# A mixer's output gates as one token-stationary block of 1024 columns

## The chip, the cores and the metric

The kernel runs on one core of a Trainium2 chip. The metric is the device time of one execution, in microseconds. The core has a matrix engine (TensorE, PE in the profile, with its weight loads as PEld), a vector engine (VectorE, DVE), a scalar engine (ScalarE, ACT), a fourth engine (GpSimd, POOL) and DMA queues that SyncE (SP) feeds. Products accumulate in PSUM and are read out by VectorE or ScalarE.

## The reference, cut to what matters

One encoder layer in fp32 over 256 tokens of width 2048: a half-step SwiGLU, a mixer, a cross-attention to 256 memory tokens, another half-step SwiGLU, a final norm. The change lies in the mixer alone:

```python
h = rms_norm(x, mix_norm[l])
proj = h @ w_in[l]                       # 2048 x 4112
u, q, k, v, g, a_lr = jnp.split(proj, list(IN_SPLITS), axis=-1)
y_pool = pool_mixer(u, pool_w[l], pool_scale[l])
y_gla = gla_mixer(q, k, v, g, a_lr, gla_w_a2[l], gla_b_a[l], gla_head_norm[l])
x = x + jnp.concatenate([y_pool, y_gla], axis=-1) @ w_out[l]
...
def gla_mixer(q, k, v, g, a_lr, w_a2, b_a, head_norm):
    ...                                  # 4 heads: scores over chunks of 64 frames, o = scores @ v
    o = o * lax.rsqrt(jnp.mean(o * o, axis=-1, keepdims=True) + RMS_EPS)
    o = o.reshape(b, s, D_GLA) * head_norm.astype(jnp.float32)
    return o.astype(dt) * jax.nn.silu(g)
```

The gates `g` are 1024 columns of `proj`, 256 for each of four heads. A head's normed output, times its gain, is multiplied by silu of its gates and becomes one eighth of the input of `w_out`.

## The kernel before, in words

**Numbers.** Every large product is made of three: weights and activations are split into a high part (`wh`, or `xh`; the first of the two parts in `xs` and `ys`) and a low part (`wl`, `xl`). For each tile of weights ScalarE casts the high part (L1607) and VectorE subtracts it to get the low part (L453, inside `low_parts`). `xs` holds the normed input of the mixer, `ys` the input of `w_out`, both as 16 tiles of 128 rows of the feature axis by 256 tokens, in two parts.

**The weight stream.** The class `Stream` keeps a list of units (one load of 1 MB of weights with its products) and of operations between them. `st.op(f, n)` puts `f` behind the n-th unit from there, or at once for n = 0. `emit` splits the weights of a unit two units ahead. Weight splits on VectorE and ScalarE keep their order (`in_turn`); other work is put among them by a list scheduler, which also moves ready instructions past others that wait.

**Forms of a block.** `block_a` (512 columns) keeps weights in the array and streams tokens: for each tile of 128 rows and each 128 columns one product of 512 columns (`wh` against both parts of the activations) and one of 256 (`wl` against the high part), both on L347. The result is transposed: features on partitions. `block_s` (1024 columns) keeps tokens in the array and streams 512 columns of weights: a pair of 128-row tiles takes 24 products of 512 columns (`unit_p`, L362), or, for the pairs in its sums, seven block products in place of eight, that is 21 (`seven`, L507). Such a pair needs more splitting: `split_seven` (L486, L280, L489, L453). Its result has tokens on partitions. Behind its last seven, `combine` (L574 to L579) adds the partial sums out of PSUM, and behind its last unit `join` (L589) adds the rest. Rows that have to have features on partitions are turned by `rows_turned` (L780): eight transposes for 512 columns.

**PSUM.** There is one pool of four tiles of two banks each (`ptile`). `block_s` holds two over the block (`open_whole`) and two more between its first seven and `combine` (`open_parts`).

**The order around the change.** Queries and keys (a `block_s`), the forget gate (`a_unit`), pool columns (two `block_a`), values V (a `block_s`, sevens at pairs 1 and 3, with `scores` of heads 0 and 1 behind its first two units), the pool group's own product (`pool_unit`, L1025), then the gates as two `block_a`. In between stand the heads' steps: `scores(h)` (decayed queries `QD`, L1155 and L1157; products, L1165; copies, L1171), `attend(h)` (L1178, L1181, L1187, L1189), `head_squares`, `head_norms(b)` (L1200) and `head_scale(b)` (L233, L1214) for each two heads. `ev_g` evicts the gates of a head: `joined` (L318, L319, L323), silu (L1221), the product with the head's output (L1223) and the split into `ys` (L285, L286). Then the block of `w_out` begins: pairs 1, 2, 3, 5, 0, 6, 4, 7 of `ys`, with sevens at pairs 0 and 4. Heads 0 to 3 are pairs 4 to 7.

Of the kernel before, what the change touches and what calls it, by code (L numbers as in the profile page):

```python
# [7 lines left out]
F32 = mybir.dt.float32  # L8
F32R = mybir.dt.float32r
AF = mybir.ActivationFunctionType  # L10
ALU = mybir.AluOpType
# [3 lines left out]
P = 128  # L15
D = 2048
S = 256
# [3 lines left out]
NB = 512  # L21
CH = 64
H = 4
# [7 lines left out]
G_FFN1, G_MIX, G_X, G_MEM, G_FFN2, G_PS, G_HN, G_BA, G_END = 0, 16, 32, 48, 64, 80, 88, 96, 100  # L31
# [68 lines left out]
def build(ctx, tc, I, out):  # L100
    nc = tc.nc
    st = Stream()
# [7 lines left out]
    scope = {"stack": None}  # L110
# [34 lines left out]
    def uid(s):  # L145
        cnt[0] += 1
        return f"{s}{cnt[0]}"

    def ctile():
        return scope["pool"].tile([P, 2, S], F32, tag="c", name=uid("c"), bufs=2)  # L150

    def ttile():
        return shared_tile("t", 2 * S, F32, uid("t"), 3).rearrange("p (a b) -> p a b", a=2)
# [27 lines left out]
    Rcol = ctl("Rcol", [P, 2])  # L181
# [8 lines left out]
    xs = main.tile([P, KT, 2, S], F32R, tag="xs", name="xs")  # L190
    ys = main.tile([P, KT, 2, S], F32R, tag="ys", name="ys")

    def gcol(i):
        return gains[:, i : i + 1]
# [102 lines left out]
    diag, rows = {}, {}  # L297
# [17 lines left out]
    def joined(ps, dst, scale=None, first=False):  # L315

        c = ctile()
        nc.scalar.copy(c, ps[:, :, S:])  # L318
        add = nc.vector.tensor_tensor(out=dst, in0=ps[:, :, :S], in1=c, op=ALU.add)  # L319
        if first:  # L320
            latest["vector"] = add
        if scale is not None:
            nc.vector.tensor_tensor(out=dst, in0=dst, in1=bc(scale), op=ALU.mult)  # L323
# [307 lines left out]
    def wblock(w, n0, k0=0, nk=KT):  # L631

        def src(k):
            return lambda raw: wload(raw.rearrange("p (k n) -> p k n", n=NB), w, k, 4, n0)
        return [src(k0 + k) for k in range(0, nk, 4)]
# [3 lines left out]
    def wwide(w, n0, k0=0, nk=KT):  # L639

        def src(k):
            def load(raw):
                raw = raw.rearrange("p (k n) -> p k n", n=2 * NB)
                if len(loaded) < 3:
                    for kk in range(2):
                        parts = (0, NB) if not loaded else (0,)
                        for c in parts:
                            n = 2 * NB // len(parts)
                            wload(raw[:, kk : kk + 1, c : c + n], w, k + kk, 1, n0 + c, n)
                else:  # L650
                    wload(raw, w, k, 2, n0, 2 * NB)
                next(first_loads, None)
                loaded.append(1)
            return load
        return [src(k0 + k) for k in range(0, nk, 2)]
# [119 lines left out]
    def rows_turned(g):  # L775

        v = four(ptile(uid("ph")))
        for i in range(4):
            for h in range(2):
                nc.tensor.transpose(  # L780
                    v[:, i, h * P : (h + 1) * P], g[:, h, i * P : (i + 1) * P], ident
                )
        return v
# [170 lines left out]
    w_in = I["w_in"][0]  # L954
    mix = {}

    def mt(name, shape, tag=None, bufs=1):
        t = whole_lines(scope["pool"], shape, F32, tag or name, uid(name), bufs)
        mix[name] = t
        return t  # L960
# [12 lines left out]
    def m4():  # L973
        return scope["pool"].tile([P, 2 * 2 * (S + PAD)], F32, tag="m4", name=uid("m4"), bufs=3)
# [164 lines left out]
        return mix["v"][:, 2 * (1 - j) + t, at : at + P]  # L1139

    def score_tile(h):
        s = mix["ST", h] = ctile() if h % 2 else mt("ST", [P, 2, S], "wa2")
        nc.gpsimd.memset(s[64:128, 0, 0:CH], 0.0)
        nc.gpsimd.memset(s[64:128, 1, 2 * CH : 3 * CH], 0.0)
        return s

    def scores(h):
        q, kd, E, F = mix["q"][:, h, :], mix["k"][:, h, :], mix["E"], mix["F"]
        e = lambda c: E[:, 4 * h + c : 4 * h + c + 1]
        f = lambda i: F[:, i, h : h + 1]  # L1150
        QD = scope["pool"].tile([P, 3 * NB], F32, tag=("xh", "xl")[h % 2], name=uid("QD"), bufs=1)
        at = (0, 3 * CH, 5 * CH)
        factors = {(0, 1): e(1), (0, 2): f(0), (0, 3): f(2), (1, 2): e(2), (1, 3): f(1), (2, 3): e(3)}
        for j in range(3):
            nc.scalar.copy(QD[:, at[j] + j * CH : at[j] + (j + 1) * CH], q[:, j * CH : (j + 1) * CH])  # L1155
            for c in range(j + 1, 4):
                nc.vector.tensor_scalar_mul(  # L1157
                    QD[:, at[j] + c * CH : at[j] + (c + 1) * CH], q[:, c * CH : (c + 1) * CH],
                    factors[j, c],
                )  # L1160
        ps = ptile(uid("pq"))
        for j in range(4):
            part = slice((j % 2) * CH, (j % 2 + 1) * CH)
            rhs = QD[:, at[j] + j * CH : at[j] + S] if j < 3 else q[:, 3 * CH :]
            nc.tensor.matmul(  # L1165
                ps[part, j // 2, j * CH : S], kd[:, j * CH : (j + 1) * CH], rhs, start=True, stop=True
            )
        s = score_tile(h)
        for j in range(4):
            part = slice((j % 2) * CH, (j % 2 + 1) * CH)  # L1170
            nc.vector.tensor_copy(s[part, j // 2, j * CH :], ps[part, j // 2, j * CH : S])  # L1171

    def attend(h):
        s = mix["ST", h]
        po = ptile(uid("po"))
        for vt in range(2):
            col = h * DV + vt * P
            nc.tensor.matmul(  # L1178
                po[:, vt, :S], v_part(0, col), s[:, 0, :], start=True, stop=False
            )  # L1180
            nc.tensor.matmul(  # L1181
                po[:, vt, 2 * CH : S], v_part(1, col), s[:, 1, 2 * CH :], start=False, stop=True
            )
        if h % 2 == 0:
            mix["oz", h // 2] = as_four(m4())
        q = mix["osq", h] = ttile()
        nc.scalar.activation(q, po[:, :, :S], AF.Square)  # L1187
        i = h % 2
        nc.vector.tensor_copy(mix["oz", h // 2][:, 2 * i : 2 * i + 2, :], po[:, :, :S])  # L1189

    def head_squares(h):
        sq = mix["osq", h]
        nc.vector.tensor_tensor(out=sq[:, 0, :], in0=sq[:, 0, :], in1=sq[:, 1, :], op=ALU.add)

    def head_norms(b):
        pn = ptile(uid("pn"))
        for i in range(2):
            sq = mix["osq", 2 * b + i]
            for t in range(2):
                nc.tensor.matmul(  # L1200
                    pn[:, 0, 2 * i + t : 2 * i + t + 1], sq[:, 0, t * P : (t + 1) * P],
                    ones[:, 0:1], start=True, stop=True,
                )
        r = mt("r", [P, 4])
        rsqrt(r, pn[:, 0, :4], DV, 4)
        mix["diag"] = [diagonal(r[:, i : i + 1]) for i in range(4)]

    def head_scale(b):
        ps = ptile(uid("ps"))
        for i in range(4):  # L1210
            spread(ps[:, i // 2, :], i % 2, mix["diag"][i])
        for i in range(2):
            oz = mix["oz", b][:, 2 * i : 2 * i + 2, :]
            nc.vector.tensor_tensor(out=oz, in0=oz, in1=bc(ps[:, i, :S]), op=ALU.mult)  # L1214

    def ev_g(b):
        def evict(p, ps):
            h = 2 * b + p
            t = ttile()
            joined(ps, t, rows["R"], b == 0)  # L1220
            nc.scalar.activation(t, t, AF.Silu)  # L1221
            for vt in range(2):
                nc.vector.scalar_tensor_tensor(  # L1223
                    out=t[:, vt, :], in0=mix["oz", b][:, 2 * p + vt, :], scalar=gcol(G_HN + 2 * h + vt),
                    in1=t[:, vt, :], op0=ALU.mult, op1=ALU.mult,
                )
            split_pair(ys, 8 + 2 * h, t)
        return evict

    for h in range(2):  # L1230
        st.op(lambda h=h: scores(h), 1 + h)
    block_s(wwide(w_in, 4 * NB), xs, qk_sums, (0, 2, 4, 5, 1, 6, 3, 7), ev_v, home=v_home)
    st.unit(load_pool, pool_unit)
    for g in range(4):
        st.op(lambda g=g: pool_out(g))
    for h in range(2):
        st.op(lambda h=h: attend(h), h)
        st.op(lambda h=h: head_squares(h), h)
        st.op(lambda h=h: scores(2 + h), h + 1)
        st.op(lambda h=h: attend(2 + h), h + 2)  # L1240
        st.op(lambda h=h: head_squares(2 + h), h + 2)
    for b in range(2):
        st.op(lambda b=b: head_norms(b), 2 + 2 * b)
        st.op(lambda b=b: head_scale(b), 3 + 2 * b)
    block_a(wblock(w_in, 6 * NB), xs, ev_g(0), (0, 0))
    block_a(wblock(w_in, 7 * NB), xs, ev_g(1))
    st.op(close_scope, 1)

    OUT_HOMES = {"T": [("kv", D, 2)], "xh": [("kv", D, 2), ("att", 3 * NB, 2)],
# [399 lines left out]
```

## Time and profile before

| | |
|---|---|
| median of 3 runs | 2077.93 us (2077.92 to 2078.28) |
| the profiled execution's own time | 2078.49 us |
| its span, first to last instruction | 2076.7 us |
| PE busy | 2064.0 us (99%) |
| DVE busy | 1833.9 us (88%) |
| ACT busy | 1158.5 us (56%) |
| POOL busy | 103.8 us (5%) |
| granted clock of TensorE | 0.999 |

The busy time of PE counts overlapping products, so the pace of a stretch is read from the chain of waits, whose rows give a start, a length and a count of instructions in a row. A row of a group gives what an instruction reads and writes, its shapes, its count, busy time and mean length, and then the idle time before it with what ended it. The table by stretches gives each engine's busy time between two moments, with its count of instructions.

### The profile page before, as it was taken

To read this page: it belongs to the slowest core of one execution; us is meant where nothing else is said; L and a number is where in the kernel's file an instruction comes from. 1 tells how busy PE (TensorE), PEld (TensorE's weight loads), DVE (VectorE), ACT (ScalarE), POOL (GpSimd) and SP (SyncE) were. 2 spreads that over 40 slices of the span, in tenths; PEclk is the share of its full clock that TensorE was granted. 3 is DMA by queue.
4 is the path that set the end of the run, shared out by engine and by line. 5 is a ranking of instruction groups with operands and counts; after the bars stand their busy time and mean duration, and the time that the engine had idled before them with its cause. 6 is when DMAs were issued, how large, how long until landed. Compare 5 with 4: busy or idle time off the path is not lost.

```text
span 2076.7 us, 24301 instructions
## 1 busy us (share of the span) xinstructions
PE 2064.0 (99%) x9585; PEld 1720.6 (83%) x9585; DVE 1833.9 (88%) x1740; ACT 1158.5 (56%) x1158; POOL 103.8 (5%) x96
## 2 busy tenths in 40 slices
PE   9999999999999999999999999999999999999998
PEld 7888888888888888888888888888888888888886
DVE  7998899989998759789889877989988999889987
ACT  7654455544555564556755554656554555545554
POOL 0000000000000000000000000000000010000001
PEclk9999999999999999999999999999999999999999
DMA  7666766566656654556755455666576765676664
GB/s 265 204 202 224 242 217 215 186 228 231 232 194 222 239 190 163 182 184 226 265 184 195 163 182 182 203 218 216 176 242 216 240 208 189 224 241 223 211 227 150
DMA packets 127083, 435.94 MB, mean 210 GB/s; under 512 B 9845, under 2 KB 13529, under 8 KB 126585
## 3 DMA queue, kind: packets, MB, share of 16 engines
q1 hardware_dynamic: 126792, 433.86, 62.6%
q8 instruction: 75, 1.23, 0.2%
q10 hardware_dynamic: 176, 0.53, 0.1%
q14 instruction: 40, 0.32, 0.0%
HBM read 417.58 MB, written 16.78 MB: 209 GB/s over the span
## 4 chain that ended last, share of the span: by engine, by line
PE 99%; DVE 0%; ACT 0%; DMA 0%; issue 0%; SPq 0%; DVEq 0%; ACTq 0%
PE pt L362 61%; PE pt L507 29%; PE pa L347 4%; PE ph L780 1%; PE pl L1343 1%; PE pv L1380 1%; PE px L791 0%; DMA x<-in_x 0%; PE pp L1025 0%; PE pe L362 0%; DVE wl L453 0%; PE po L1178 0%; PE pa L1052 0%; PE tm L1290 0%; PE px L717 0%; PE pq L1165 0%
## 5 line engine op out<-in xcount | busy, mean ns | idle before, releaser
L362 PE MATMUL pt<-wh,xs 128*128 128x512 f32 x2272 | 729.2, 390 | 0.4 <-ACT xs L236 0.4
L1607 ACT CAST wh<-raw 128x2048 fp32r<-128x2048 f32 x247 | 471.6, 1912 | 254.3 <-PE pt L362 119.3
L453 DVE TENSOR_TENSOR wl<-raw,wh 128x2048 fp32r<-128x2048 f32 (+1 forms) x247 | 527.6, 2143 | 95.0 <-ACT wh L1607 94.7
L362 PEld LDWEIGHTS pt<-wh,xs 128*128 128x128 f32 x2272 | 425.8, 188 | 88.2 <-ACT xs L236 0.7
L489 ACT CAST wh<-T 128x1024 fp32r<-128x1024 f32 x254 | 266.8, 1054 | 383.9 <-DVE T L486 374.3
L362 PE MATMUL pt<-wh,ys 128*128 128x512 f32 x1440 | 454.7, 389 | 0.0
L362 PE MATMUL pt<-wl,xs 128*128 128x512 f32 x1136 | 442.9, 390 | 0.0
L362 PEld LDWEIGHTS pt<-wh,ys 128*128 128x128 f32 x1440 | 270.2, 188 | 55.8
L453 DVE TENSOR_TENSOR wl<-T,wh 128x2048 fp32r<-128x2048 f32 (+1 forms) x127 | 285.2, 2246 | 2.5 <-ACT wh L489 2.2
L362 PE MATMUL pt<-wl,ys 128*128 128x512 f32 x720 | 280.7, 390 | 0.2 <-DVE wl L453 0.2
L362 PEld LDWEIGHTS pt<-wl,xs 128*128 128x128 f32 x1136 | 213.4, 188 | 43.4 <-DVE wl L280 0.2
L280 DVE TENSOR_TENSOR xl<-raw,xh 128x1536 fp32r<-128x1536 f32 x127 | 222.3, 1750 | 13.6 <-ACT xh L279 13.4
L279 ACT CAST xh<-raw 128x1536 fp32r<-128x1536 f32 x127 | 188.0, 1480 | 62.4 <-PE pt L507 42.3
L486 DVE TENSOR_TENSOR T<-T,raw 128x512 f32<-128x512 f32 x254 | 175.2, 690 | 6.6
L362 PEld LDWEIGHTS pt<-wl,ys 128*128 128x128 f32 x720 | 135.2, 188 | 28.4 <-DVE wl L453 0.6
L486 DVE TENSOR_TENSOR T<-raw 128x1024 f32<-128x1024 f32 x127 | 154.6, 1217 | 0.5
L457 POOL TENSOR_TENSOR wl<-raw,wh 128x768 fp32r<-128x768 f32 x44 | 81.7, 1856 | 1449.9 <-DVE wl L453 1427.1
L507 PE MATMUL pt<-wh,xs 128*128 128x512 f32 x384 | 149.2, 389 | 0.0
L507 PE MATMUL pt<-xh,xs 128*128 128x512 f32 x392 | 146.2, 389 | 0.0
L507 PE MATMUL pt<-wh,xe 128*128 128x512 f32 x320 | 124.3, 389 | 0.0
L347 PE MATMUL pa<-xs,wh 128*128 128x512 f32 x256 | 91.5, 401 | 0.0
L507 PEld LDWEIGHTS pt<-xh,xs 128*128 128x128 f32 x392 | 73.6, 188 | 15.2
(259 smaller groups left out, 2276.5 us busy)
## 6 DMA issues: line engine op xcount, KB each, us to landing
raw<-in_ffn_w_down SPq DMA_DIRECT2D x88, 1024.0 KB, 5.4
raw<-in_ffn_w_up SPq DMA_DIRECT2D x80, 1024.0 KB, 5.0
raw<-in_ffn_w_gate SPq DMA_DIRECT2D x77, 1024.0 KB, 5.1
raw<-in_w_in SPq DMA_DIRECT2D x32, 1024.0 KB, 5.1
raw<-in_xattn_w_kv SPq DMA_DIRECT2D x32, 1024.0 KB, 5.0
raw<-in_w_out SPq DMA_DIRECT2D x16, 1024.0 KB, 5.5
raw<-in_xattn_w_q SPq DMA_DIRECT2D x16, 1024.0 KB, 5.5
raw<-in_xattn_w_o SPq DMA_DIRECT2D x16, 1024.0 KB, 5.5
```

The source lines that it names most:

```text
L279: in_turn("scalar", lambda: nc.scalar.copy(hi, src))
L280: in_turn("vector", lambda: nc.vector.tensor_tensor(out=lo, in0=src, in1=f32(hi), op=ALU.subtract))
L347: nc.tensor.matmul(o, w, x, start=k == 0 and i == 0, stop=last and i == 1)
L362: nc.tensor.matmul(ps, a, w, start=first and i == 0, stop=last and i == 2)
L453: in_turn("vector", lambda: nc.vector.tensor_tensor(out=lo[:, :n], in0=src[:, :n], in1=f32(hi[:, :n]), op=ALU.subtract))
L457: rest = nc.gpsimd.tensor_tensor(out=lo[:, n:], in0=src[:, n:], in1=f32(hi[:, n:]), op=ALU.subtract)
L486: in_turn("vector", lambda: nc.vector.tensor_tensor(out=o, in0=a, in1=b, op=ALU.add))
L489: in_turn("scalar", lambda: nc.scalar.copy(th[:, c], t[:, c]))
L507: nc.tensor.matmul(banks[n], x, w, start=n in fresh and j == 0, stop=n in ends and j == 2)
L780: nc.tensor.transpose(v[:, i, h * P : (h + 1) * P], g[:, h, i * P : (i + 1) * P], ident)
L1343: nc.tensor.matmul(ps[:, t, :M], ys[:, 4 * h + d, a, tok], xa["K", h][:, d, b, :], start=i == 0, stop=i == 11,)
L1607: in_turn("scalar", lambda: nc.scalar.copy(hi, raw))
```

## The change

The two `block_a` of the gates become one `block_s` of 1024 columns with the same order and the same sevens (pairs 1 and 3) as V's block. Its rows get their factor and silu at once on ScalarE, with tokens on partitions (`ev_g`), and after the first unit of `w_out` they are turned (`gate`), and each head's output is multiplied by them out of PSUM and split into `ys`. The heads' work is placed otherwise: `scores` of heads 2 and 3 stand behind V's block and ahead of the pool unit, with `QD` and the score tiles in other buffers (`m4`, and half each of a tile of the tag `T`); all four `attend`, the norms and the scales stand before or in the first three units of the gates.

```diff
--- before.py
+++ after.py
@@ -1139,7 +1139,13 @@
         return mix["v"][:, 2 * (1 - j) + t, at : at + P]
 
     def score_tile(h):
-        s = mix["ST", h] = ctile() if h % 2 else mt("ST", [P, 2, S], "wa2")
+        if h < 2:
+            s = ctile() if h else mt("ST", [P, 2, S], "wa2")
+        else:
+            if h == 2:
+                mix["two"] = scope["pool"].tile([P, 4 * NB], F32, tag="T", name=uid("ST"), bufs=1)
+            s = mix["two"][:, (h - 2) * NB : (h - 1) * NB].rearrange("p (a b) -> p a b", a=2)
+        mix["ST", h] = s
         nc.gpsimd.memset(s[64:128, 0, 0:CH], 0.0)
         nc.gpsimd.memset(s[64:128, 1, 2 * CH : 3 * CH], 0.0)
         return s
@@ -1148,7 +1154,9 @@
         q, kd, E, F = mix["q"][:, h, :], mix["k"][:, h, :], mix["E"], mix["F"]
         e = lambda c: E[:, 4 * h + c : 4 * h + c + 1]
         f = lambda i: F[:, i, h : h + 1]
-        QD = scope["pool"].tile([P, 3 * NB], F32, tag=("xh", "xl")[h % 2], name=uid("QD"), bufs=1)
+        QD = m4() if h >= 2 else scope["pool"].tile(
+            [P, 3 * NB], F32, tag=("xh", "xl")[h], name=uid("QD"), bufs=1
+        )
         at = (0, 3 * CH, 5 * CH)
         factors = {(0, 1): e(1), (0, 2): f(0), (0, 3): f(2), (1, 2): e(2), (1, 3): f(1), (2, 3): e(3)}
         for j in range(3):
@@ -1213,37 +1221,40 @@
             oz = mix["oz", b][:, 2 * i : 2 * i + 2, :]
             nc.vector.tensor_tensor(out=oz, in0=oz, in1=bc(ps[:, i, :S]), op=ALU.mult)
 
-    def ev_g(b):
-        def evict(p, ps):
-            h = 2 * b + p
-            t = ttile()
-            joined(ps, t, rows["R"], b == 0)
-            nc.scalar.activation(t, t, AF.Silu)
+    def ev_g(j, c):
+        for h in range(2):
+            nc.scalar.activation(c[:, h, :], c[:, h, :], AF.Silu, scale=Rcol[:, h : h + 1])
+        mix["gate", j] = c
+
+    def gate(b):
+        v = rows_turned(mix["gate", b])
+        for p in range(2):
+            h, t = 2 * b + p, ttile()
             for vt in range(2):
                 nc.vector.scalar_tensor_tensor(
-                    out=t[:, vt, :], in0=mix["oz", b][:, 2 * p + vt, :], scalar=gcol(G_HN + 2 * h + vt),
-                    in1=t[:, vt, :], op0=ALU.mult, op1=ALU.mult,
+                    out=t[:, vt, :], in0=mix["oz", b][:, 2 * p + vt, :],
+                    scalar=gcol(G_HN + 2 * h + vt), in1=v[:, 2 * p + vt, :],
+                    op0=ALU.mult, op1=ALU.mult,
                 )
             split_pair(ys, 8 + 2 * h, t)
-        return evict
 
     for h in range(2):
         st.op(lambda h=h: scores(h), 1 + h)
     block_s(wwide(w_in, 4 * NB), xs, qk_sums, (0, 2, 4, 5, 1, 6, 3, 7), ev_v, home=v_home)
+    for h in (2, 3):
+        st.op(lambda h=h: scores(h))
     st.unit(load_pool, pool_unit)
     for g in range(4):
         st.op(lambda g=g: pool_out(g))
-    for h in range(2):
-        st.op(lambda h=h: attend(h), h)
-        st.op(lambda h=h: head_squares(h), h)
-        st.op(lambda h=h: scores(2 + h), h + 1)
-        st.op(lambda h=h: attend(2 + h), h + 2)
-        st.op(lambda h=h: head_squares(2 + h), h + 2)
+    for h in range(H):
+        st.op(lambda h=h: attend(h), h // 2)
+        st.op(lambda h=h: head_squares(h), h // 2)
     for b in range(2):
-        st.op(lambda b=b: head_norms(b), 2 + 2 * b)
-        st.op(lambda b=b: head_scale(b), 3 + 2 * b)
-    block_a(wblock(w_in, 6 * NB), xs, ev_g(0), (0, 0))
-    block_a(wblock(w_in, 7 * NB), xs, ev_g(1))
+        st.op(lambda b=b: head_norms(b), 1 + b)
+        st.op(lambda b=b: head_scale(b), 2 + b)
+    block_s(wwide(w_in, 6 * NB), xs, qk_sums, (0, 2, 4, 5, 1, 6, 3, 7), ev_g, home=wide_home)
+    for b in range(2):
+        st.op(lambda b=b: gate(b), 1)
     st.op(close_scope, 1)
 
     OUT_HOMES = {"T": [("kv", D, 2)], "xh": [("kv", D, 2), ("att", 3 * NB, 2)],
```

## The prediction

> **What bounds the kernel now.** I read the page first, then the chain of waits over the mixer, then the table by stretches, and last the groups of VectorE in each stretch. The page says that the matrix engine sets the time, at full clock:
>
> ```profile
> span 2076.7 us, 24301 instructions
> PE 2064.0 (99%) x9585; PEld 1720.6 (83%) x9585; DVE 1833.9 (88%) x1740; ACT 1158.5 (56%) x1158; POOL 103.8 (5%) x96
> PE 99%; DVE 0%; ACT 0%; DMA 0%; issue 0%; SPq 0%; DVEq 0%; ACTq 0%
> ```
>
> So an edit is worth what it does to PE's own work, plus any wait it puts before PE. Idle PE can't be won: in the whole stretch from 700 to 1100 us PE has only these waits:
>
> ```profile
> PE pt L507 <- DVE xl L280: 0.2, 1, 0.2
> PE pt L362 <- DVE wl L453: 0.2, 1, 0.2
> ```
>
> The table by stretches shows how near the second engine is (columns: PE, PEld, DVE, ACT, POOL busy, clock, DMA share, GB/s):
>
> ```profile
> 804.60:848.90 44.30, 44.30 (x205) 36.01 (x204) 42.17 (x57) 21.12 (x22) 2.50 (x6) 1.00 0.57 187
> 854.50:910.30 55.80, 55.80 (x339) 48.83 (x338) 38.62 (x65) 29.96 (x32) 0.23 (x2) 1.00 0.50 164
> 910.30:932.10 21.80, 21.80 (x97) 18.02 (x97) 19.92 (x25) 13.80 (x14) 0.00 (x0) 1.00 0.68 221
> ```
>
> They are V's block, the gates with the heads' work, and the first four units of `w_out`. VectorE has 2.1 us free in V's block, 17.2 in the gates and 1.9 at the start of `w_out`.
>
> **The gates' products.** The old form takes 2 blocks x 16 row tiles x 4 column groups x 2 = 256 products. All of them are in these eight pieces of the chain (start, length, count):
>
> ```profile
> 855.05 1.73 PE pa L347 x10
> 857.66 9.54 PE pa L347 x54
> 869.50 3.02 PE pa L347 x17
> 873.83 1.88 PE pa L347 x11
> 876.50 4.44 PE pa L347 x24
> 883.14 2.10 PE pa L347 x12
> 886.92 11.71 PE pa L347 x66
> 899.52 10.75 PE pa L347 x62
> ```
>
> Their sum is 45.17 us, or 0.353 for a product of 512 with one of 256. The new form takes six pairs of 24 and two of 21: 186 products of 512. V's block is the same thing with the same order. It lies between the first of these rows and the start of the pool products, with two groups of score products in it:
>
> ```profile
> 804.63 5.46 PE pt L362 x24
> 810.09 0.79 PE pq L1165 x6
> 816.56 0.80 PE pq L1165 x6
> 848.87 5.75 PE pp L1025 x48
> 910.27 21.80 PE pt L362 x96
> ```
>
> 848.87 - 804.63 - 0.79 - 0.80 = 42.65 us. At the undisturbed pace of the last row, 21.80 / 96 = 0.2271 us, 186 products make 42.24. I take 42.65, since V's block carries the same sevens. The gain is 45.17 - 42.65 = **2.52 us** (2.93 at the other end).
>
> The Trainium skill, "TensorE: Matmul & The Clock Gate", Back-to-back issue gap, puts a warm product of N columns at N / 2.4 + 2.5 ns. As an estimate from it, the old 128 couples would take 41.6 us and the new 186 products 40.1, a gain of 1.5 us, which the transposes below would more than eat at their measured price. The trace disagrees on size: 227 ns for 512 columns, and 353 for a couple where the formula says 325.
>
> **The turning.** `gate` adds 16 transposes of fp32 rows. The same 16 stand in the chain for the queries and keys:
>
> ```profile
> 755.68 0.11 PE ph L780
> 756.49 0.76 PE ph L780 x7
> 762.11 0.87 PE ph L780 x8
> ```
>
> That is **1.74 us** on PE, which nothing can hide, for PE has no free time. The heads' own products (scores, attend, norms, scales) are the same in number and shape and only move, so they cost PE nothing by themselves. PE's balance is -2.52 + 1.74 = **-0.8 us** (-1.2 at the other end).
>
> **VectorE and ScalarE.** The rows that price the edit:
>
> ```profile
> L453 DVE TENSOR_TENSOR wl<-T,wh 128x2048 fp32r<-128x2048 f32 x2 | 4.6, 2286 | 0.1
> L280 DVE TENSOR_TENSOR xl<-raw,xh 128x1536 fp32r<-128x1536 f32 x2 | 3.5, 1753 | 0.0
> L453 DVE TENSOR_TENSOR wl<-raw,wh 128x1280 fp32r<-128x1280 f32 x2 | 3.0, 1482 | 0.0
> L486 DVE TENSOR_TENSOR T<-T,raw 128x512 f32<-128x512 f32 x4 | 2.8, 688 | 0.0
> L486 DVE TENSOR_TENSOR T<-raw 128x1024 f32<-128x1024 f32 x2 | 2.4, 1216 | 0.0
> L589 DVE TENSOR_TENSOR v<-pt,v 128x1024 f32<-128x1024 f32 x2 | 2.3, 1214 | 0.0
> L319 DVE TENSOR_TENSOR t<-pa,c 128x512 f32<-128x512 f32 x3 | 2.1, 687 | 1.4 <-ACT c L318 1.4
> L323 DVE TENSOR_TENSOR t<-t,R 128x512 f32<-128x512 f32 x2 | 1.4, 688 | 0.0
> L1223 DVE SCALAR_TENSOR_TENSOR t<-m,gains,t 128x256 f32<-128x256 f32 x4 | 1.8, 479 | 1.2 <-ACT t L1221 1.2
> L286 DVE TENSOR_TENSOR ys<-t,ys 128x512 fp32r<-128x512 f32 x2 | 1.4, 688 | 0.1
> ```
>
> Each seven adds 1.216 + 2 x 0.688 + 1.753 = 4.3 us of VectorE, 8.7 for two, in a stretch where 17.2 are free; these are hidden. The four L319 and four L323 go (-5.5 us); `combine` and two joins come (0.69 + 1.22 + 0.69 as in V's block, + 2.43 = 5.0). Silu moves from turned halves to rows, four instructions as before, and ScalarE has 25.8 us free in the stretch.
>
> What is tight is the start of `w_out`. Before, the gates of heads 2 and 3 were evicted there; after, those of all four. On VectorE this removes 2 x 0.687 + 2 x 0.688 = 2.75 us and adds four L1223 (1.92), two L286 (1.38) and two joins (2.43), less 2.286 - 1.482 = 0.80 for the unit whose low part GpSimd shares. The net is +2.2 us against 1.9 us free plus the 1.74 us by which the transposes lengthen the stretch. That leaves 1.4 us: I take no stall, with 0 and 2 us as ends. A gain is excluded, since PE does not wait there now.
>
> **The handover from V to the pool product.** Score products of heads 2 and 3 now come first. They take two of the four PSUM tiles, the two that `combine` frees, where today the pool product finds them:
>
> ```profile
> 849.59 2.35 DVE L589 TENSOR_TENSOR v<-pt,v 128x1024 f32<-128x1024 f32 x2
> ```
>
> The pool product then needs a tile that a join frees: the first is free at 849.59 + 1.18 = 850.77, while PE has done V and two score groups at 848.87 + 1.59 = 850.46. That is a wait of **0.3 us**, if the operands of the scores are ready. The lower end is 0; the upper is worked out below. A gain is excluded, as no wait stands there now. `QD` is cast from `q` and could be built during V's second half, once the pool sums have left the `m4` buffers.
>
> **The sum.** -2.52 + 1.74 + 0.3 + 0 = -0.5 us. The profiled execution's own time is 2078.49, 1.8 more than its span, and it would become 2078.0; against the median of 2077.93, 0.56 lower, it is **2077.4 us**. A measurement of this kernel can tell about 0.2% (4.2 us) from no change, so the forecast is no change.
>
> **The rivals.**
>
> *A. The handover queues up on VectorE* (slower). Between V's last product and the first free tile for the gates' first unit VectorE may have to do, in line: joins 2.35, two low parts (1.48 + 2.29), the copies of two heads' scores, which are these four for one head, 1.33 us, twice; eight L240; two heads' copies out of PSUM at 0.69; and the 12 multiplications of `QD`:
>
> ```profile
> 868.05 1.33 DVE L1171 COPY ST<-pq 64x256 f32<-64x256 f32 x4 [5.28 <-PE pq L1165]
> L240 DVE SCALAR_TENSOR_TENSOR ys<-pp,gains,ys 128x256 fp32r<-128x256 f32 x8 | 3.6, 478 | 0.8 <-ACT ys L236 0.8
> L1157 DVE TENSOR_SCALAR QD<-q,F 128x64 f32<-128x64 f32 x6 | 2.9, 515 | 0.0
> L1157 DVE TENSOR_SCALAR QD<-q,E 128x64 f32<-128x64 f32 x6 | 1.5, 247 | 1.0 <-PE pt L507 1.0
> 868.00 0.63 PE po L1178 x2
> ```
>
> Together: 2.35 + 3.77 + 2.66 + 3.6 + 1.4 + 4.4 = 18.2 us. PE's cover is 1.6 (scores) + 5.75 (pool) + two heads' attend, each from 868.00 to the gates' products at 869.50, 3.0: 10.3 us. If all stands in line, PE waits 7.9 us: 2077.93 - 0.8 + 7.9 = **2085.0 us**. It is slower by over 0.2% from 5 us of wait on. For it: four PSUM tiles are all held for a moment. Against it: the scheduler moved gate products between the parts of `attend` at 855.05, so it fills such gaps, and only half of the L240 stand before the first free tile. The Trainium skill, "Perfetto Trace Analysis", Identifying Performance Opportunities, says that repeated gaps on the saturated engine can mean too few buffers; no run here shows such a gap yet. I give A 0.13.
>
> *B. The start of `w_out` stalls.* The seven of pair 0 needs its split, 1.216 + 1.38 + 1.753 + 2.286 = 6.6 us of VectorE, before the fifth unit. If the work of heads 2 and 3 (2 x (0.96 + 0.69) = 3.3 us) goes ahead of it, or holds its buffer, the 1.4 us of spare time are exceeded by 1.9: 2077.4 + 1.9 = **2079.3 us**. For it: 90% of that stretch is VectorE's already. Chance 0.20, within 0.2%.
>
> *C. PE gains more than counted*, as where the old products lost more around the heads' work than the chain shows. The best that rows allow is -1.2 us, **2076.7 us**; over 4.2 us would need another 3 us out of work that only moves. Chance of that: 0.03.
>
> **How the numbers follow.** Forecast 0.61, B 0.20, A 0.13, C's large gain 0.03, and 0.03 for a reordered schedule later in the kernel that costs over 4.2 us. Faster 0.03, same 0.61 + 0.20 = 0.81, slower 0.13 + 0.03 = 0.16. The range runs from 2075.5, where PE's best balance of -1.2 is doubled to allow for a later stretch reordered to advantage, to 2081.2, a third of the way from B's 2079.3 to A's 2085.0. It leaves out most of A, the reordered schedule and the large gain, some 2 in 10.
>
> **What would show it.** Right: 186 products L362 and L507 for the gates in 42.2 to 42.7 us, 16 more L780 near 0.109 us apiece, no wait of PE over 0.5 us between 845 and 935, and `w_out` starting 1 to 3 us earlier. A shows as PE waiting for DVE L589, L1171 or L240 near 850 to 860; B as PE L507 waiting for DVE L280 or L453 some 22 us into `w_out`. The forecast is wrong if the span moves by over 4.2 us, or if PE's gaps in this region add up to more than 2 us.

## The result, and the profile after

The changed kernel takes 2084.99 us (median of 7 runs, 2084.49 to 2087.4), the kernel before 2078.01 us in the runs beside it (7 runs, 2077.92 to 2079.64). The ratio is 1.0034, with a 95% interval of 1.0022 to 1.0046: slower by 7 us, where -0.5 had been forecast.

The page of the changed kernel, to be held against the first lines of the prediction:

```profile
span 2083.2 us, 24193 instructions
PE 2066.3 (99%) x9531; PEld 1719.5 (83%) x9531; DVE 1839.0 (88%) x1745; ACT 1158.0 (56%) x1157; POOL 107.5 (5%) x98
```

PE is as full as before by its share; the loss has to be read from its waits. One is new, and one has grown from the 0.2 us that the prediction shows (in all, times, longest):

```profile
PE pt L362 <- DVE m L1197: 3.4, 1, 3.4
PE pt L362 <- DVE wl L453: 1.7, 1, 1.7
```

The first stands at the handover from V to the gates. The chain of waits there (start, length, what):

```profile
848.51 1.44 PE pq L1173 x11
849.96 5.96 PE pp L1025 x48
...
856.31 1.90 ACT wh L1618
...
858.23 2.29 DVE wl L453
860.52 0.79 DVE ys L240 x2
861.31 0.61 DVE m L1197
...
861.96 9.15 PE pt L362 x32
```

The score products and the pool product follow V at once. PE then makes the products of `attend` for heads 0 and 1, which take 2.60 us. The last row of them ends at 858.13 + 0.38 = 858.51:

```profile
858.13 0.38 PE L1189 MATMUL po<-c,v 128*128 128x128 f32 x2
```

The gates' first product starts at 861.96. In between ScalarE casts a weight, VectorE subtracts its low part, and only then copies out of PSUM (L240, L1197).

Behind the wait the pace is wrong too: 32 products in 9.15 us, where 0.2271 us each make 7.27. Here are the start of that row in the timeline of PE, and the table by stretches (the column before the last two is the granted clock):

```profile
861.96 0.51 PE L362 MATMUL pt<-wh,xs 128*128 128x512 f32 x1 [3.44 <-DVE m L1197]
...
862.70 1.05 PE L362 MATMUL pt<-wh,xs 128*128 128x512 f32 x2
863.55 0.63 PE L362 MATMUL pt<-wl,xs 128*128 128x512 f32 x1
```

```profile
860.00:864.00 4.00, 2.04 (x6) 1.61 (x7) 3.96 (x9) 0.87 (x3) 0.00 (x0) 0.79 0.56 173
864.00:868.00 4.00, 4.00 (x16) 3.21 (x15) 0.48 (x1) 0.47 (x1) 0.00 (x0) 0.78 0.22 89
868.00:872.00 4.00, 4.00 (x20) 3.41 (x19) 0.00 (x0) 0.81 (x1) 0.00 (x0) 1.00 0.00 0
```

The two products of the second row start 0.85 us ahead of the next one, so each takes 0.425 us. The clock in the stretches from 860 to 868 is 0.79 and 0.78, and it is back at 1.00 from 868 on.

Further down the chain:

```profile
921.94 1.75 PE ph L780 x16
...
937.07 2.72 PE pt L507 x12
...
972.04 2.21 DVE wl L453
...
974.30 5.29 PE pt L362 x22
```

**Where 6.5 us of span went.** V's first product starts at 804.28 (804.63 before), and `w_out`'s first seven at 937.07 (932.08 before). The stretch is 5.34 us longer. In it are the wait, 3.45; the slow clock, 9.15 - 7.27 = 1.88; the transposes, 1.75; the other products of the gates and of the first four units of `w_out`, 65.5 against 45.17 + 21.80 = 67.0, so -1.45; and -0.3 in the heads' and pool's products. A second loss of 1.53 us stands in `w_out`'s second block, at the wait for L453 that ends at 974.30. The rest of the kernel, shifted, is the same.

### The profile page after: what moved, and what is told of

It is laid out like the page before. It is cut to its first block, busy times and chain, and to the rows that moved or that the text cites. A ratio compares the mean times of both kernels' runs of the same rounds, so it can differ in the third digit from the quotient of the medians.

```text
span 2083.2 us, 24193 instructions
## 1 busy us (share of the span) xinstructions
PE 2066.3 (99%) x9531; PEld 1719.5 (83%) x9531; DVE 1839.0 (88%) x1745; ACT 1158.0 (56%) x1157; POOL 107.5 (5%) x98
## 4 chain that ended last, share of the span: by engine, by line
PE 98%; DVE 1%; ACT 0%; DMA 0%; issue 0%; SPq 0%; DVEq 0%; ACTq 0%
PE pt L362 62%; PE pt L507 29%; PE pa L347 2%; PE ph L780 1%; PE pl L1354 1%; PE pv L1391 1%; PE px L791 1%; DVE wl L453 0%; PE pp L1025 0%; PE pe L362 0%; DMA x<-in_x 0%; PE pa L1052 0%; PE tm L1301 0%; PE px L717 0%; PE pq L1173 0%
## 5 line engine op out<-in xcount | busy, mean ns | idle before, releaser
L362 PE MATMUL pt<-wh,xs 128*128 128x512 f32 x2368 | 761.1, 391 | 3.5 <-DVE m L1197 3.4
L453 DVE TENSOR_TENSOR wl<-raw,wh 128x2048 fp32r<-128x2048 f32 (+1 forms) x245 | 521.5, 2137 | 98.8 <-ACT wh L1618 98.3
L362 PEld LDWEIGHTS pt<-wh,xs 128*128 128x128 f32 x2368 | 444.5, 188 | 95.7 <-DVE m L1197 3.6
L362 PE MATMUL pt<-wl,xs 128*128 128x512 f32 x1184 | 462.3, 391 | 0.0
L453 DVE TENSOR_TENSOR wl<-T,wh 128x2048 fp32r<-128x2048 f32 (+1 forms) x129 | 289.9, 2247 | 2.8 <-ACT wh L489 2.4
L362 PEld LDWEIGHTS pt<-wl,xs 128*128 128x128 f32 x1184 | 222.7, 188 | 45.4
L280 DVE TENSOR_TENSOR xl<-raw,xh 128x1536 fp32r<-128x1536 f32 x129 | 226.0, 1752 | 14.5 <-ACT xh L279 14.4
L507 PE MATMUL pt<-wh,xs 128*128 128x512 f32 x388 | 150.8, 389 | 0.0
L507 PEld LDWEIGHTS pt<-wh,xs 128*128 128x128 f32 x388 | 72.8, 188 | 15.1
```

The lines of the kernel that those rows point to most:

```text
L280: in_turn("vector", lambda: nc.vector.tensor_tensor(out=lo, in0=src, in1=f32(hi), op=ALU.subtract))
L362: nc.tensor.matmul(ps, a, w, start=first and i == 0, stop=last and i == 2)
L453: in_turn("vector", lambda: nc.vector.tensor_tensor(out=lo[:, :n], in0=src[:, :n], in1=f32(hi[:, :n]), op=ALU.subtract))
L507: nc.tensor.matmul(banks[n], x, w, start=n in fresh and j == 0, stop=n in ends and j == 2)
```

## The experiments

Theory T was that the heads' new place takes the PSUM tiles from the gates; the rival R, that the new form of the gates costs the time itself.

**e1: the form alone.** The heads' steps in their old order, score tiles as before.

```diff
-    for h in (2, 3):
-        st.op(lambda h=h: scores(h))
...
-    for h in range(H):
-        st.op(lambda h=h: attend(h), h // 2)
...
+    for h in range(2):
+        st.op(lambda h=h: attend(h), h)
...
+        st.op(lambda h=h: scores(2 + h), h + 1)
+        st.op(lambda h=h: attend(2 + h), h + 2)
...
```

> The gates in their new form, with the heads' steps in the order of before and their score tiles as before. Theory T (held tiles): the loss comes from the heads' new place, which gives the two free PSUM tiles at the end of the pool product to attend of heads 0 and 1, so that the gates' first unit waits 3.45 us, and TensorE's clock falls for some 4 us behind that wait (1.9 us more). Without it there is no wait over 1 us near 850 to 870 and the time is 2077.0 to 2079.7 us (PE's balance of -0.8, and up to 2.5 us for late splits). Rival R (the form): two more sevens and their splits cost the time themselves; 2083 us or more here.

Measured: 2080.48 us, ratio 1.0013 (1.0003 to 1.0023). The wait and the slow clock are gone; the gates' products run on between the parts of `attend`:

```profile
854.66 2.31 PE pt L362 x10
856.97 0.22 PE po L1183 x2
...
857.85 10.02 PE pt L362 x44
```

So R falls for most of the loss. But 2080.48 lies over T's range by 0.8 us, and over PE's balance by some 3 us. The trace shows 1.8 us of it as short waits of PE between 845 and 980: 0.6 for the norms (L212), 0.6 for L453, 0.3 for L280 and 0.3 for L1191.

**e2: the heads' move alone.** The gates as two `block_a`, with `ev_g` of before.

```diff
-    block_s(wwide(w_in, 6 * NB), xs, qk_sums, (0, 2, 4, 5, 1, 6, 3, 7), ev_g, home=wide_home)
+    block_a(wblock(w_in, 6 * NB), xs, ev_g(0), (0, 0))
+    block_a(wblock(w_in, 7 * NB), xs, ev_g(1))
```

> The heads' steps in their new place, the gates in the old form (two blocks of 512 columns, weights in the array). T: the same two tiles are taken by attend, so PE waits 2 to 3.5 us at the start of the gates and the granted clock falls behind it: 2078.0 + 3.45 + 1.9 = 2083.3 us. R: no loss without the form, 2078 us.

Measured: 2084.01 us, ratio 1.0028 (1.0017 to 1.0039). The same wait, behind the same copy, with the old products behind it, and the clock down again:

```profile
PE pa L347 <- DVE m L1197: 3.4, 1, 3.4
```

```profile
860.00:864.00 4.00, 1.86 (x5) 1.59 (x6) 4.00 (x9) 0.96 (x3) 0.00 (x0) 0.71 0.50 141
864.00:868.00 4.00, 4.00 (x21) 3.48 (x20) 0.63 (x2) 0.47 (x1) 0.00 (x0) 0.87 0.31 121
```

The heads' move makes most of the loss (6 us of 7) without the new form. In this run 1.0 us of it is a wait for L228, and there is no wait for L453 in the second block.

**e4: the wait filled with work.** The products of head 1's `attend` are made three times over.

```diff
-        for vt in range(2):
+        for vt in [0, 1] * (3 if h == 1 else 1):
```

> The changed kernel with the products of attend of head 1 made three times over (same values), 2.6 us of work in the wait. T: the wait shrinks from 3.45 us to about 0.9, the products behind it run at 0.227 us instead of some 0.29, and the time falls by the clock's share alone, to 2083.1 us. Rival to the clock's share: the slow pace has another cause (weights, PSUM), stays as it is, and the time is 2085 us or more.

Measured: 2083.18 us, ratio 1.0025 (1.0015 to 1.0035), 1.8 us under the changed kernel. The wait for L1197 is 0.8 us, and behind it 33 products take 0.236 us each:

```profile
PE pt L362 <- DVE m L1197: 0.8, 1, 0.8
```

```profile
862.21 7.79 PE pt L362 x33
```

2.6 us of useless work made the kernel faster. The intervals of the two ratios overlap, but none of these runs (2082.86 to 2084.03) reaches those of the changed kernel (from 2084.49 on), and the rows show the pace. So the clock's share is shown, by its size.

**e3: the gates' first unit ahead of `attend`.** On TensorE's queue `attend` is held behind that unit, and the later steps come one unit later.

```diff
+        with tc.issue_after(latest["tensor"].ins):
...
-        st.op(lambda h=h: attend(h), h // 2)
...
+        st.op(lambda h=h: attend(h), 1 + h // 2)
...
```

The first line stands around the products of `attend`.

> The changed kernel with attend of heads 0 and 1 held behind the gates' first unit on TensorE's queue, and the later steps of the heads one unit later. T: the first unit takes the two free tiles, the wait of 3.45 us and the slow clock go, 2085.0 - 5.3 = 2079.7 us. R: still 2084 us or more, as the form is untouched.

Measured: 2089.33 us, ratio 1.0053 (1.0038 to 1.0068); a miss by 9.6 us. The place is right and the time wrong. The gates do start at once, and the loss stands 25 us later:

```profile
855.76 10.91 PE pt L362 x48
...
879.93 1.24 DVE T L488
```

From 879.91 to 890.82 the chain is VectorE's and ScalarE's. PE waits there three times (2.0, 0.6 and 1.3 us), and the clock behind it is 0.65 in the stretch from 892 to 896. The buffer `T`, which the split of the first seven needs, holds the score tiles of heads 2 and 3 until the last `attend`.

**e6: e3 with the score tiles out of T**, and the squares of heads 2 and 3 in an `m4` buffer.

> The kernel of e3 (attend behind the gates' first unit), with the score tiles of heads 2 and 3 out of the buffer T that the sevens' splits need (heads' squares in another buffer to make room). If e3's 2089 us came from that buffer, held until attend of the last head, its PE waits near 880 to 891 go (some 9 us) and the time is 2080 to 2081 us. Rival: attend standing later is itself the cost, through PSUM; 2087 us or more.

Measured: 2083.17 us, ratio 1.0024 (1.0015 to 1.0034). The wait goes and 6.2 us come back, so the buffer was e3's main cause; 2 us more than expected remain, at the wait for L228 that e5 shows best (2.1 us here, with a clock of 0.57 from 896 to 900).

**e5: two heads' outputs in one PSUM tile.** Of the two free tiles one is left for the gates.

```diff
-    def attend(h):
...
+    def attend(b):
         po = ptile(uid("po"))
...
+        for i in range(2):
+            h, s, c = 2 * b + i, mix["ST", 2 * b + i], i * S
...
```

> The changed kernel, with the outputs of attend of two heads in one PSUM tile (each head half of both banks), everything else in the same order. T: of the two free tiles at the end of the pool product one is left for the gates' first unit, so the wait of 3.45 us and the slow clock behind it go: 2085.0 - 5.3 = 2079.7 us, no wait over 1 us there. Rival Q (the line on VectorE): the readers of PSUM are late whatever tile they read, the gates' second half of a unit waits as long, and the time stays at 2083 us or more.

Measured: 2082.95 us, ratio 1.0025 (1.0015 to 1.0034). T's place is right: 48 products of the gates follow `attend` at once and at full pace. VectorE copies the first tile out as late as before (at 862.04, 2.7 us behind the gates' first product), so Q's reason falls, though the time that it named came: a free tile is what was missing. But only 2.0 of 5.3 us came back in the time, and 2.95 in the stretch from V's first product to `w_out`. Most of the rest turned into a wait further on:

```profile
859.33 10.92 PE pt L362 x48
...
892.17 0.91 PE ps L233 x8
...
893.10 1.28 DVE m L1224 x2
...
895.60 0.30 DVE diag L228
...
896.04 0.46 PE ps L233 x2
```

```profile
892.00:896.00 4.00, 1.85 (x17) 1.75 (x15) 2.43 (x9) 0.20 (x1) 0.00 (x0) 1.00 0.00 0
```

The second scale's products (`ps`) stand on TensorE's queue ahead of the sevens' and wait for a chain of small steps on VectorE and ScalarE. PE's last product before, one of the norm's (`pn`), ends at 893.85, so PE is idle for 2.19 us up to 896.04. The Trainium skill, "TensorE: Matmul & The Clock Gate", Part 2, says that matmuls stay in program order and only weight loads are pulled ahead; the trace agrees in that no product runs in this gap. The first scale and the norm also hold PSUM tiles until about 894.4, and how much of the wait is theirs was not taken apart.

The clock stays at 1.00 over this wait. In e7, the next experiment, the same wait is just as long, but the six products behind it take 2.41 us where they take 1.38 in e5, and the clock is 0.88 and 0.69:

```profile
PE ps L233 <- DVE diag L228: 2.2, 1, 2.2
```

```profile
896.36 2.41 PE pt L507 x6
```

```profile
892.00:896.00 4.00, 1.81 (x16) 1.75 (x15) 2.88 (x11) 0.21 (x1) 0.00 (x0) 0.88 0.00 0
896.00:900.00 4.00, 4.00 (x17) 3.16 (x16) 0.56 (x2) 2.33 (x3) 0.00 (x0) 0.69 0.00 0
```

So the length of a wait does not by itself tell whether the clock falls. The Trainium skill, "TensorE: Matmul & The Clock Gate", Part 1, has the clock halved after an idle window of about 3.4 us, which runs freely. The half pace agrees: behind the wait of 3.45 us the products stood 0.425 us apart, against 0.227 at full clock. The 3.4 us of idleness do not: in e7 PE was idle for 2.19 us, or 3.1 with the norm's eight products of one column ahead of it.

**e7: e5 with less work on VectorE at the start of `w_out`.**

```diff
-            split_pair(ys, 8 + 2 * h, t)
+            if h < 2:
+                split_pair(ys, 8 + 2 * h, t)
+            else:
+                nc.scalar.copy(ys[:, 8 + 2 * h : 10 + 2 * h, 0, :], t)
```

The kernel leaves out the low parts of heads 2 and 3 of the input of `w_out`, 1.4 us of VectorE.

> The kernel of e5 without the low parts of heads 2 and 3 of the input of w_out (left out of the computation): 1.4 us less on VectorE at the start of w_out. Theory B (VectorE's line there, +2.2 us of work, is carried to the second block of w_out): the PE wait of 1.7 us behind L453 there shrinks to about 0.2 and the time falls by 1.4 us from e5's. Rival: that wait is an accident of ScalarE's order (L248 ahead of L285) and stays; no difference to e5 over 0.4 us.

Measured: 2081.69 us, ratio 1.0018 (1.0009 to 1.0026), 1.26 us under e5. The intervals overlap, and the clock fell in one of the two profiles only, so the rows have to decide. The wait for L453 in the second block, 1.7 us in e5, is 0.2 us here:

```profile
PE pt L362 <- DVE wl L453: 0.2, 1, 0.2
```

So the second loss goes with 1.4 us of VectorE's work. But e7 also changes the order on the engines. In the changed kernel VectorE is idle twice ahead of that low part, each time for ScalarE:

```profile
954.24 2.29 DVE L453 TENSOR_TENSOR wl<-raw,wh 128x2048 fp32r<-128x2048 f32 x1 [1.31 <-ACT wh L1618]
971.55 0.29 DVE L286 TENSOR_TENSOR ys<-j,ys 128x128 fp32r<-128x128 f32 x1 [0.96 <-ACT ys L285]
```

In e7 VectorE does a step of `combine` (L576) in the first gap, and the second is 0.33 us, for ScalarE makes L285 ahead of L248 there. The rival in the expectation, ScalarE's order, is therefore not excluded.

**e8: e5 with the norms behind the gates' seventh unit and the scales behind the eighth.** As built, heads 0 and 1 are scaled with the factors of heads 2 and 3; the work is the same.

> The kernel of e5 with the heads' norms and scales behind the gates' seventh unit (and head 3's square in another buffer), so that the sevens find their two PSUM tiles at once. Theory S (the sevens' products stand apart because pn and ps hold a tile, and the second seven's split is late for it): the gates' 186 products take V's 42.65 us instead of about 1 us more, 1.0 us under e5. Rival: the norms' 5.6 us of VectorE move to where it is short, at the start of w_out, and the time is 1 to 3 us over e5's.

Measured: 2088.54 us, ratio 1.0051 (1.0038 to 1.0063). Both the theory and its rival are seen, but the rival had 1 to 3 us over e5, and it is 5.6. The sevens stand together: 48 products in 10.92 us and 138 between 872.29 and 903.63, 42.3 for 186. The norms' chain then stops PE for 9.7 us, and the clock is 0.50 from 908 to 916:

```profile
PE ps L233 <- DVE diag L228: 9.7, 1, 9.7
```

**e9 and e10: norms early, scales late.** The norms of both head pairs stand behind the gates' first unit (e9) or its first two (e10), with diagonals in tiles of their own, and the second scale (e9) or both (e10) behind the seventh unit.

```diff
-        st.op(lambda b=b: head_norms(b), 1 + b)
-        st.op(lambda b=b: head_scale(b), 2 + b)
+        st.op(lambda b=b: head_norms(b), (1, 2)[b])    # e9: (1, 1)
+        st.op(lambda b=b: head_scale(b), (7, 7)[b])    # e9: (2, 7)
```

> The kernel of e5 with the norms of heads 2 and 3 one unit earlier and their scale (the products L233) behind the gates' seventh unit, in tiles of their own so that nothing waits for the first scale. Theory H (products of a norm stand at the head of TensorE's queue while VectorE and ScalarE still work out their diagonals, 2.2 us of wait and some 0.8 around it in e5): no PE wait for DVE L228 over 0.5 us, 2082.95 - 3.0 = 2080.0 us or a little less; what is left above 2078 is the wait of 1.7 us in the second block of w_out. Rival: the wait goes to the second scale or into w_out, 2082 us or more.

> As e9, with both scales behind the seventh unit and the norms where the change has them. H: the diagonals are ready long before, no wait for L228, and the sevens stand together, so 2079.5 to 2080 us; e8's 9.7 us wait (norms and scales both late) goes. Rival: the four L1222-like products of 0.64 us that scale the heads now stand at the start of w_out on VectorE, which lengthens the wait there by 1 to 2 us: 2081 to 2082 us.

Measured: e9 2078.09 us, ratio 1.0000 (0.9991 to 1.0009); e10 2077.16 us, ratio 0.9997 (0.9988 to 1.0006). Neither has a wait for L228, and both are faster than expected: with it went the second seven's late split, and the wait for L453 fell to 0.6 us, though no work was left out. The gates' products of e10 in the chain:

```profile
858.55 10.92 PE pt L362 x48
...
872.88 7.64 PE pt L362 x33
...
880.86 3.56 PE pt L362 x15
...
884.76 3.55 PE pt L507 x15
888.31 4.08 PE pt L362 x18
892.39 1.36 PE pt L507 x6
893.75 1.36 PE pt L362 x6
895.11 4.76 PE pt L507 x21
899.87 5.44 PE pt L362 x24
```

They are 186 products in 42.67 us. e10 is the best version, 7.8 us under the changed kernel, and not told apart from the kernel before.

## Why the prediction was wrong

**PE's balance was right.** It had 42.65 us for the gates' products and 1.74 for the turning, -0.8 in all, and so some 2077.2 us without waits; e10 has 42.67, 1.75 and 2077.16. That the times meet within 0.1 us is luck, as e10 still waits 0.6 us for L453. That e10 stands below the kernel before is not shown, only that it isn't slower by more than 0.06%.

**The step that failed is the handover.** It put 0.3 us, for the tile that the pool product needs. That product came without a wait. What was not asked is which tile the *gates'* first unit gets: both that the score copies free go to `attend`, which stands ahead in the queue, and the pool product holds the other two. In e5 `attend` leaves one of them, and the wait is gone. Rival A had this place and, by chance, the time: its 7.9 us of wait had `QD` in the line, 4.4 us. `QD` was built from 830.30 on, during V's second half, as the forecast's own text had it; the row of head 3's first part:

```profile
834.75 0.25 DVE L1165 TENSOR_SCALAR m<-q,E 128x64 f32<-128x64 f32 x1
```

Without it A's sum is 18.2 - 4.4 - 10.3 = 3.5 us, and 3.45 was measured. That this hits so well is luck too: in the trace only five of the eight L240 and one of the two copies stand before the end of the wait, and VectorE waits 1.3 and 0.6 us for ScalarE, which A did not have. The place and the held tiles are what A had right. The argument against A, that the scheduler fills such gaps with gate products, held only while a tile was free for them (e1, e5). A's chance of 0.13 was too low, as the sum without `QD` needed no mishap.

**A cost had no term: the clock.** The forecast and its rivals took TensorE's pace as constant. The wait of 3.45 us cost 1.88 more behind it, and e4 measured this share as 1.8.

**B named the engine, but not the place, and was no rival.** It was priced at 1.9 us, at the first seven of `w_out`. There the split was just in time; PE waited for VectorE 35 us later, in the second block, with 1.53. It was given as an alternative to A, and came on top of it.

**"No stall" inside the gates was wrong by 1.1 us.** The products gained 1.45 instead of 2.52, with the heads' norms and scales among the sevens; e8 shows the products whole, at 42.3, without them. Whether the PSUM tile that the norms hold or the late split of the second seven costs it was not taken apart. In e5 the same place became the next bound, a wait of 2.2 us.

The sum as it should have been: -0.8 + 3.5 + 1.9 + 1.1 + 1.5 = 7.2 us, and 7.0 was measured.

Why the wait for L453 fell in e9 and e10, the traces show: the order changed. Up to the low part before it (960.29 in e10, 966.73 in the changed kernel) both take 29.7 us from the first seven of `w_out`, so VectorE is no earlier (e7 and the kernel before take 28.5). From there to the awaited low part e10 takes 4.11 us and the changed kernel 5.23, as L286, which waits for ScalarE, stands behind it in e10. What stays open is how much of the second loss is VectorE's added work and how much the order.

## What to carry to other kernels

When steps are moved on a full matrix engine, count PSUM tiles at each boundary: who holds each, who is next in the queue for the free ones, and which reader on which engine frees the next. Ask the same of small products that wait for a chain on other engines, since everything behind them on the queue waits too; start the chain early and place its products late. Removing one wait gives back only as much as the next one leaves: here 2.0 us came back of 5.3. And when a wait is to be explained, look at the order on the engine that ends it, not only at its load.

## What the hardware showed unexpected

A wait of 3.45 us on TensorE lost 1.88 us again, with a clock of 0.79 and 0.78 in the stretches from 860 to 868. Filling the wait with 2.6 us of repeated products left 0.8 us of it, kept the clock at 1.00 and gained 1.8 us.

The length of the wait does not settle whether the clock falls: behind the same 2.19 us it stayed at 1.00 in e5 and was 0.88 and 0.69 in e7. The size of a fall did repeat. Counted as lost full-speed time it was (0.21 + 0.22) x 4 = 1.72 us in the changed kernel, 1.68 in e2, 1.72 in e6 and 1.72 in e7, and 5.1 over the 9.7 us of e8, three times as much. What decides between a fall and none is not shown.
